# Weighted sums of two attentions with tokens on partitions, and a mask added by matmul

## The chip, the core and the metric

The kernel runs on one core of a Trainium2 chip, and the whole computation, two different network blocks one after the other, is one launch. A core has a matrix engine (TensorE: PE for the matmuls and PEld for its weight loads in the profile), a vector engine (DVE), a scalar engine (ACT), GpSimd (POOL) and a sync engine (SP) that here mostly issues DMAs. They run side by side, each through its own list of instructions in a fixed order, and wait for each other by semaphores. The metric is the device time of one execution, in microseconds (us); lower is better.

## The reference

All is in float32 with 256 tokens of width 1024. The first block (two layers of a pooling, a sparse-attention and a memory branch with mixture of experts) is touched by the change in one buffer count only. The second block has two layers; in each, a projection z = rms(x) w_in feeds three mixers whose outputs stand side by side and go through w_out, followed by a feed-forward part:

```python
# swa, 8 heads of 64 (2 heads of keys and values): window and causal by chunks of 64, with sinks
s = where(allowed, q k^T / 8, -inf);  m = max(max(s), sink);  p = exp(s - m)
ya = (p / (sum(p) + exp(sink - m))) v
# fox, 4 heads of 64: softmax attention with forget gates F
s = where(kpos <= qpos, q k^T / 8 + F_q - F_k, -inf);  yb = softmax(s) v
# mlstm, 4 heads of 64, the gated memory: by chunks in the reference
Dm = where(causal, b_t - b_s + i_s, -inf);  m_t = max(inter, max(Dm))
h = ((q k^T * exp(Dm - m_t)) v + old state) / max(|den|, exp(-m_t))
x = x + concat([ya, yb, rms(h) * gate]) @ w_out
x = x + square(relu(rms(x) @ w_ff1)) @ w_ff2
```

## The kernel before, in words

The 256 tokens are two blocks of 128, one per step of the loops over `b` (`NB` is 2). Activations have tokens on the 128 partitions; what a dense product needs is turned by PE transposes (a matmul with the identity) so that the contraction is on partitions. Dense products are done in two halves of each number: `split` makes a rounded high part `wh` and a rest `wl` of a weight (L99 and L100, or L104 and L105 with a gain), `transposed` (L174 to L177) and `split_out` (L286, L287) do the same with activations, and `mm3` multiplies high by high (L111), high weight rest by high (L112) and the rest of the activations by high (L113).

In the second block (`second_layer`, from L1228) a layer goes: the projections in pieces (`project`), the gated memory (`mlstm`, L1482 to L1545), swa (L1349 to L1386), fox (L1446 to L1479), then `w_out` with the eight blocks of input rows in the order `ks=(6, 0, 2, 4)`: the gated memory's rows first, swa's next, fox's last. With `early=True` the last parts run all of token block 0 before block 1 (`TAIL = 3`). Then the residual is added (L1270), x is turned (L174) and the feed-forward part follows. The order of the instructions on an engine is not written out: a tile scheduler orders them when the program is built, and puts dense products that are ready between the steps of the mixers.

For each token block, swa first makes the scores of all heads (L371), and one fused DVE instruction per head (L1362) adds the mask, writes the masked scores to SBUF and leaves the row's maximum. In a second loop, for each pair of heads, ACT takes the exponentials (L1380) with their sums; `over_sum` (L1388 to L1395) adds the sink's term (L1392), takes the reciprocals (L1393) and multiplies both heads' rows by them (L1395); and `weighted` (L375 to L387) turns the normalised rows with PE (L381), copies them to SBUF (L383, on ACT, or on DVE for the second pair of fox) and multiplies (L386). There a value block of 128 keys x 64 is the stationary operand and the turned probabilities stream, so that the sums come out with the head's 64 columns on partitions, two heads in one 128-partition tile: what `w_out` needs. `split_out` writes them to `yh` and `yl` (tiles named `big`). fox does the same with four heads, scores at L1460 and L1463, maxima at L1467 and exponentials at L1474. Token block 0 has 128 keys (one block of keys), token block 1 has 256 (two).

The gated memory already has its sums with tokens on partitions: transposes L1522, copy L1524, and L1529, where the turned weights are the stationary operand and the 64 value columns stream. L1533 multiplies by the reciprocal denominators, and after the norm, whose chain runs over ACT, DVE and POOL (L1198 to L1203, L1538, L1540), two transposes (L1543) turn the result back. Its exponents come from matmuls whose mask and maxima are the fused instruction at L1501, one for each head.

## Time and profile before

| | us |
|---|---|
| runs of the kernel before | 1623.46, 1632.21, 1632.83 (median 1632.21) |
| the profiled execution | 1629.87 |
| its span in the trace | 1628.1 |
| the granted clock of PE, mean over the span | 0.988 |
| second block | from about 1008 to the end |

The profile is of one execution. Its span reaches from the first instruction to the last, and 1.77 us of the execution lie around it. A row of a timeline gives a start and a length in us; successive matmuls overlap at their ends, so what a matmul costs on PE is the distance to the next start. A matmul in float32 appears as two records. "Idle before" and the name behind the arrow tell how long the engine had nothing to do and which instruction ended that.

### The profile page before, as it was taken

How to read it: one execution, taken by the hardware profiler on the slowest of the kernel's cores; microseconds unless marked ns; L12 is line 12 of the kernel's file. 1: busy time of each engine (PE TensorE's matmuls, PEld its weight loads, DVE VectorE, ACT ScalarE, POOL GpSimd, SP SyncE). 2: the span in 40 equal slices, each digit the busy share in tenths (PEclk: the TensorE clock that was granted, in tenths of full speed). 3: DMA queues.
4: the chain of work that ended last, by engine and by line, in shares of the span. 5: the costliest groups of instructions: out<-in, count | busy, mean ns of one | idle time of the engine just before them, and what ended most of it. 6: DMA issues, size and time to landing. Idle time of an engine off the chain costs nothing.

```text
span 1628.1 us, 24829 instructions
## 1 busy us (share of the span) xinstructions
PE 1584.0 (97%) x9844; PEld 1187.8 (73%) x9844; DVE 872.5 (54%) x1818; ACT 694.7 (43%) x1178; POOL 83.4 (5%) x97
## 2 busy tenths in 40 slices
PE   8999999999999999999999998999999999899998
PEld 7877998444436987999534344866988987688897
DVE  5587557411114687556512124787565568765554
ACT  5545544301003645544310012666555556655553
POOL 1000012000000000011000001130000000100000
PEclk9999999999999998999999999999999999999999
DMA  9553776899999652686899998623555554245550
GB/s 316 182 175 104 282 271 229 349 408 409 408 409 336 205 179 101 242 303 235 313 409 409 409 409 303 222 81 109 204 182 181 171 180 142 74 160 185 190 189 33
DMA packets 162560, 394.71 MB, mean 242 GB/s; under 512 B 15716, under 2 KB 21860, under 8 KB 162436
## 3 DMA queue, kind: packets, MB, share of 16 engines
q1 hardware_dynamic: 157184, 384.98, 64.8%
q0 software_dynamic: 2144, 6.91, 1.3%
q8 instruction: 78, 1.28, 0.3%
q10 hardware_dynamic: 3108, 1.16, 0.3%
q14 instruction: 46, 0.38, 0.1%
HBM read 391.97 MB, written 1.05 MB: 241 GB/s over the span
## 4 chain that ended last, share of the span: by engine, by line
PE 43%; DVE 4%; DMA 1%; ACT 1%; POOL 1%; issue 0%; SPq 0%; POOLq 0%; ACTq 0%; DVEq 0%
PE a L1016 7%; PE d L112 6%; PE d L111 6%; PE d L113 6%; PE a L111 4%; PE a L112 4%; PE a L113 4%; PE a L1037 3%; PE a L956 1%; DMA raw<-in_w_in_dram 1%; DVE wl L105 1%; PE d L1050 1%; DVE sall L1362 1%; PE a L386 1%; PE a L381 0%
## 5 line engine op out<-in xcount | busy, mean ns | idle before, releaser
L100 DVE TENSOR_TENSOR wl<-raw,wh 128x1024 fp32r<-128x1024 f32 (+1 forms) x232 | 284.0, 1226 | 220.2 <-ACT wh L99 219.6
L99 ACT CAST wh<-raw 128x1024 fp32r<-128x1024 f32 (+1 forms) x232 | 240.2, 1038 | 245.9 <-PE d L112 133.7
L111 PE MATMUL d<-big,wh 128*128 128x256 f32 (+1 forms) x976 | 277.7, 285 | 2.0 <-ACT big L176 1.1
L112 PE MATMUL d<-big,wh 128*128 128x256 f32 (+1 forms) x976 | 277.2, 284 | 1.8 <-DVE big L177 1.8
L113 PE MATMUL d<-big,wl 128*128 128x256 f32 (+1 forms) x976 | 275.7, 284 | 0.0
L105 DVE SCALAR_TENSOR_TENSOR wl<-raw,gcols,wh 128x512 fp32r<-128x512 f32 (+1 forms) x224 | 151.8, 713 | 76.4 <-ACT wh L104 76.0
L111 PEld LDWEIGHTS d<-big,wh 128*128 128x128 f32 (+1 forms) x976 | 186.1, 191 | 5.2 <-ACT big L176 1.8
L112 PEld LDWEIGHTS d<-big,wh 128*128 128x128 f32 (+1 forms) x976 | 186.1, 191 | 4.5 <-DVE big L177 2.4
L104 ACT ACTIVATE wh<-raw,gcols 128x512 fp32r<-128x512 f32 (+1 forms) x224 | 143.7, 687 | 104.6 <-PE a L113 39.1
L111 PE MATMUL d<-wh,big 128*128 128x512 f32 (+1 forms) x480 | 188.2, 393 | 0.0
L112 PE MATMUL d<-wl,big 128*128 128x512 f32 (+1 forms) x480 | 187.0, 390 | 1.1 <-DVE wl L105 0.9
L113 PE MATMUL d<-wh,big 128*128 128x512 f32 (+1 forms) x480 | 187.1, 390 | 0.2 <-DVE big L177 0.2
L113 PEld LDWEIGHTS d<-big,wl 128*128 128x128 f32 (+1 forms) x976 | 185.7, 191 | 0.4 <-issue 0.3
L1016 PE MATMUL a<-raw,xg 128*64 128x512 f32 x832 | 182.9, 592 | 0.0
L1016 PEld LDWEIGHTS a<-raw,xg 128*64 128x64 f32 x832 | 59.9, 137 | 118.1 <-issue 109.5
L1021 DVE TENSOR_TENSOR sl<-sl,a 128x512 f32<-128x512 f32 x16 | 11.0, 688 | 189.1 <-PE a L1016 172.8
L1037 PE MATMUL a<-raw,sl 128*64 128x512 f32 x480 | 107.0, 595 | 0.7 <-ACT sl L1028 0.7
L112 PEld LDWEIGHTS d<-wl,big 128*128 128x128 f32 x480 | 92.3, 192 | 18.0 <-DVE wl L105 1.5
L113 PEld LDWEIGHTS d<-wh,big 128*128 128x128 f32 x480 | 92.1, 192 | 18.2 <-issue 1.4
L111 PEld LDWEIGHTS d<-wh,big 128*128 128x128 f32 x480 | 92.2, 192 | 17.8 <-issue 2.0
L111 PE MATMUL a<-wh,s 128*128 128x512 f32 x256 | 101.3, 396 | 0.0
L112 PE MATMUL a<-wl,s 128*128 128x512 f32 x256 | 101.2, 395 | 0.0
(415 smaller groups left out, 2240.3 us busy)
## 6 DMA issues: line engine op xcount, KB each, us to landing
raw<-in_w_dram SPq DMA_DIRECT2D x328, 512.0 KB, 10.2
raw<-in_w_in_dram SPq DMA_DIRECT2D x64, 1024.0 KB, 6.3
raw<-in_w_ff_dram SPq DMA_DIRECT2D x64, 1024.0 KB, 5.4
br<-in_w_dram SPq DMA_DIRECT2D x36, 512.0 KB, 10.2
raw<-in_w_out_dram SPq DMA_DIRECT2D x16, 1024.0 KB, 5.1
raw<-in_w_br_dram SPq DMA_DIRECT2D x12, 1024.0 KB, 6.6
raw<-in_w_mem_kv_dram SPq DMA_DIRECT2D x7, 1024.0 KB, 11.6
gate<-in_w_dram SPq DMA_DIRECT2D x12, 512.0 KB, 10.2
```

The source lines that it names most:

```text
L99: nc.scalar.copy(hi, src)
L100: nc.vector.tensor_tensor(lo, src, hi, OP.subtract)
L104: nc.scalar.activation(hi[:, k], src[:, k], AF.Copy, scale=g)
L105: nc.vector.scalar_tensor_tensor(lo[:, k], src[:, k], g, hi[:, k], OP.mult, OP.subtract)
L111: mm(ps, sh, mh, start=start, stop=False)
L112: mm(ps, sh, ml, start=False, stop=False)
L113: mm(ps, sl, mh, start=False, stop=stop)
L386: nc.tensor.matmul(po[64 * e:64 * e + 64], value(e, k), pT[:, e, k], start=(k == 0), stop=(k == b))
L956: mm(ps[:, kk], part(b, k + kk), s[:, b], start=(i == 0), stop=(i == len(terms) - 1))
L1016: mm(ps[64 * a:64 * a + 64], g_[:, k, 64 * a:64 * a + 64], w[i][k // 2][:, a, k % 2], start=(k == 0), stop=(k == 7))
L1037: mm(pss[h][64 * a:64 * a + 64], hT[:, k, 64 * a:64 * a + 64], w[k][:, a, h], start=(k == 0), stop=(k == 3))
L1050: mm(acc[2 * b + h], sT[:, b * P:b * P + P], ys[h][:, i], start=False, stop=(p == 7 and i == 1))
```

## The change

In swa and fox, `weighted` gives way to `weighted_rows`: the exponentials are turned as they are, without the normalisation, and the turned rows become the stationary operand (128x128) with the 64 value columns streaming (L406 in the changed kernel), as in the gated memory. The sums of all heads then stand side by side with tokens on partitions, and `heads_out` takes the reciprocals of all the sums at once (L411), multiplies once for all heads (L413), turns the result in pieces of 128 columns (L417: four for swa, two for fox) and hands them to `split_out`. swa adds its sink terms once per token block. In the gated memory, a causal mask in bf16 is added to the diagonal 128 columns of each head's exponents by a matmul with a bf16 identity (L385, 8 per layer); one reduction per bank (L392) takes the maxima of the two heads in it; and the exponentials read the bank. The first block's tile of probabilities `p` has 3 buffers instead of 4. Some constants are also cast to bf16, among them copies that nothing reads.

```diff
-        p = self.t(pool, [P, S], F32, "p", 4)[:, :n]
+        p = self.t(pool, [P, S], F32, "p", 3)[:, :n]
...
+    def add_mask(self, sc, mask):
+
+        w = mask.shape[1]
+        for ps in sc:
+            m, n = ps.shape[1:]
+            for h in range(m):
+                self.nc.tensor.matmul(ps[:, h, n - w:], self.ident16, mask, start=False, stop=(h == m - 1))
+
+    def maxima(self, sc, N, tag):
+
+        m = sc[0].shape[1]
+        mx = self.t(N, [P, 2, m], F32, tag, 2)
+        for e in range(2):
+            self.nc.vector.tensor_reduce(mx[:, e], sc[e], AX.X, OP.max)
+        return mx
+
+    def weighted_rows(self, po, pr, b, pool, value, alt=False):
...
+        for e in range(2):
+            for k in range(b + 1):
+                nc.tensor.transpose(pt[:, e, k], pr[e][:, k * P:k * P + P], self.ident)
+        pT = self.t(pool, [P, 2, 2, P], F32, "pT", 2)[:, :, :b + 1]
+        (nc.vector.tensor_copy if alt else nc.scalar.copy)(pT, pt)
+        for e in range(2):
+            for k in range(b + 1):
+                nc.tensor.matmul(po[:, e], pT[:, e, k], value(e, k), start=(k == 0), stop=(k == b))
+
+    def heads_out(self, po, sm, heads, hi, lo, N):
+
+        nc = self.nc
+        nc.vector.reciprocal(sm, sm)
+        y = self.t(N, [P, 512], F32, "row2", 2)[:, :heads * 64]
+        nc.vector.tensor_tensor(y.rearrange("p (h d) -> p h d", d=64), po,
+                                sm[:, :, None].to_broadcast([P, heads, 64]), OP.mult)
+        ps = self.psa().rearrange("p (k c) -> p k c", k=4)
+        for k in range(heads // 2):
+            nc.tensor.transpose(ps[:, k], y[:, k * P:k * P + P], self.ident)
+        self.split_out(ps[:, 0:heads // 2], hi, lo)
...
-                self.over_sum(s[:, g], sm[:, g], sks[b][:, g])
                 v0 = 640 + 64 * (j // 2)
-                self.weighted(po[:, j], [s[:, 2 * j], s[:, 2 * j + 1]], b, N,
-                              lambda e, k: z[:, k, v0:v0 + 64])
-            self.split_out(po, yh[:, 0:4, cols], yl[:, 0:4, cols])
...
+                self.weighted_rows(po[:, 2 * j:2 * j + 2], [s[:, 2 * j], s[:, 2 * j + 1]], b, N,
+                                   lambda e, k: z[:, k, v0:v0 + 64])
+            nc.vector.tensor_tensor(sm, sm, sks[b], OP.add)
+            self.heads_out(po, sm, 8, yh[:, 0:4, cols], yl[:, 0:4, cols], N)
...
-                self.over_sum(s[:, g], sm[:, g])
-                self.weighted(po[:, j], [s[:, 2 * j], s[:, 2 * j + 1]], b, N,
-                              lambda e, k: z[:, k, 1280 + 64 * (2 * j + e):][:, :64], j == 1)
-            self.split_out(po[:, 0:2], yh[:, 4:6, cols], yl[:, 4:6, cols])
+                self.weighted_rows(po[:, 2 * j:2 * j + 2], [s[:, 2 * j], s[:, 2 * j + 1]], b, N,
+                                   lambda e, k: z[:, k, 1280 + 64 * (2 * j + e):][:, :64], j == 1)
+            self.heads_out(po, sm, 4, yh[:, 4:6, cols], yl[:, 4:6, cols], N)
...
-                                     start=True, stop=True)
+                                     start=(j == 0), stop=False)
+            self.add_mask(sc, self.causal)
+            nm = self.maxima(sc, N, "cmx")
+            nc.vector.tensor_scalar(nm, nm, 0.0, -1.0, OP.max, OP.mult)
...
-                nc.vector.tensor_tensor_reduce(s[:, h], sc[h % 2][:, h // 2], self.cz[:, S - n:], 1.0, 0.0,
-                                               OP.add, OP.max, mx[:, h:h + 1])
...
-                nc.scalar.activation(s[:, h], s[:, h], AF.Exp, bias=mx[:, h:h + 1])
+                nc.scalar.activation(s[:, h], sc[h % 2][:, h // 2], AF.Exp, bias=nm[:, h % 2, h // 2:][:, :1])
```

The change moves dense products on PE. The first place is layer 2, from the end of swa's scores into the weighted sums of its first token block. A row is the line, the operation, out<-in, the size, and a count where it repeats; `d` are the banks of dense products, `sall` the exponentials of swa. Before:

```order
L113 MATMUL d_21936<-wh_21954,big_20839 128x512
L111 MATMUL d_21936<-wh_21954,big_20838 128x512
L381 MATMUL a_21675<-ident,sall_4388_21611 128x128 x2
L112 MATMUL d_21936<-wl_21955,big_20838 128x512
L113 MATMUL d_21936<-wh_21954,big_20839 128x512
L111 MATMUL d_21937<-wh_21954,big_20838 128x512
L112 MATMUL d_21937<-wl_21955,big_20838 128x512
L386 MATMUL a_21667<-pT_21678,z_20807 64x128 x2
```

And in the changed kernel:

```order
L373 MATMUL a_21658<-akT_21496,s_4346_21377 128x256
L113 MATMUL d_21926<-wh_21930,big_20841 128x512
L111 MATMUL d_21926<-wh_21930,big_20840 128x512
L401 MATMUL a_21677<-ident,sall_4398_21617 128x128
L112 MATMUL d_21926<-wl_21931,big_20840 128x512
L113 MATMUL d_21926<-wh_21930,big_20841 128x512
L401 MATMUL a_21677<-ident,sall_4398_21617 128x128
L111 MATMUL d_21927<-wh_21930,big_20840 128x512
L112 MATMUL d_21927<-wl_21931,big_20840 128x512
L113 MATMUL d_21927<-wh_21930,big_20841 128x512
L406 MATMUL a_21673<-z_20809,pT_21680 128x64 x2
```

Between the last score and the first transposes 14 dense products stood before, of which the last two are shown; now two stand there. The other twelve stand further on.

The second place is layer 2, the end of fox's second token block (`sh` are its exponentials, `row` the product of `heads_out`, `x` the residual after `w_out`). Before:

```order
L386 MATMUL a_21873<-pT_21902,z_20807 64x128 x4
L381 MATMUL a_21913<-ident,sh_21874 128x128 x4
L112 MATMUL d_21936<-wl_22027,big_20838 128x512
L113 MATMUL d_21936<-wh_22026,big_20839 128x512
L111 MATMUL d_21936<-wh_22026,big_20838 128x512
L112 MATMUL d_21936<-wl_22027,big_20838 128x512
L113 MATMUL d_21936<-wh_22026,big_20839 128x512
L386 MATMUL a_21873<-pT_21918,z_20807 64x128 x4
L112 MATMUL d_21937<-wl_22019,big_20838 128x512
L113 MATMUL d_21937<-wh_22018,big_20839 128x512
```

And in the changed kernel:

```order
L406 MATMUL a_21865<-z_20809,pT_21891 128x64 x4
L401 MATMUL a_21899<-ident,sh_21866 128x128 x4
L406 MATMUL a_21865<-z_20809,pT_21904 128x64 x4
L417 MATMUL a_21913<-ident,row_4469_21911 128x128 x2
L174 MATMUL a_22064<-ident,x_17744 128x128 x4
L111 MATMUL d_21927<-wh_22014,big_20840 128x512
L112 MATMUL d_21927<-wl_22015,big_20840 128x512
L111 MATMUL d_21929<-wh_22018,big_20840 128x512
L113 MATMUL d_21927<-wh_22014,big_20841 128x512
```

Five dense products stood between the last transposes and their sums, and 17 behind the sums, the first five of which take no rows of fox. Now none stands between, and the 12 behind (four are shown) all take fox's rows of the second token block.

## Rows read from the trace of the kernel before

**Rows 1.** From the page: PE's line of the first part (busy us, share of the span, instructions), and the clock granted to it in 40 slices of the span, in tenths of full speed.

```profile
PE 1584.0 (97%) x9844; PEld 1187.8 (73%) x9844; DVE 872.5 (54%) x1818; ACT 694.7 (43%) x1178; POOL 83.4 (5%) x97
...
PEclk9999999999999998999999999999999999999999
```

**Rows 2.** Windows of the second block, one per row: start and end in us from the span's start, length; then busy us and instructions of PE, PEld, DVE, ACT and POOL in this order; the mean granted clock; the busy share of the DMA engines; GB/s. 1000 to 1020 is the start of the second block; 1049 to 1077 and 1349 to 1382 hold the gated memory of layers 1 and 2, 1077 to 1137 and 1382 to 1442 their two attentions.

```profile
1000.00:1020.00 20.00, 14.42 (x59) 11.07 (x56) 16.11 (x30) 12.10 (x20) 5.21 (x9) 0.83 0.51 169
1049.00:1077.00 28.00, 26.83 (x153) 21.04 (x151) 23.88 (x81) 16.70 (x36) 5.63 (x9) 1.00 0.35 118
1077.00:1137.00 60.00, 54.86 (x340) 39.89 (x341) 45.40 (x156) 39.92 (x99) 8.52 (x8) 1.00 0.26 90
1349.00:1382.00 33.00, 30.99 (x172) 23.75 (x170) 27.05 (x95) 18.92 (x41) 2.11 (x2) 1.00 0.36 127
1382.00:1442.00 60.00, 54.76 (x340) 39.42 (x341) 44.75 (x154) 39.66 (x98) 9.40 (x6) 1.00 0.27 88
```

**Rows 3.** What PE waited for from 1020 to 1136 (layer 1): PE's line and tile, the engine, line and tile waited for; us in total, how often, the longest.

```profile
PE a L381 <- DVE sall L1395: 1.9, 3, 0.9
...
PE a L1543 <- DVE chn L1540: 0.8, 1, 0.8
```

**Rows 4.** The same view from 1318 to 1442 (layer 2).

```profile
PE a L381 <- DVE sall L1395: 2.0, 3, 0.9
PE a L1543 <- DVE chn L1540: 1.4, 2, 0.9
```

**Rows 5.** Timeline of PE, layer 2, from the end of swa's scores (L371) into its weighted sums: start in us, us, engine, line, operation, out<-in, size, count, and in brackets the idle time before and what ended it. A 128x128 f32 matmul with 64 or 128 columns leaves two records.

```profile
1397.06 0.50 PE L113 MATMUL d<-wh,big 128*128 128x512 f32 x1
...
1397.63 0.39 PE L112 MATMUL d<-wl,big 128*128 128x512 f32 x1
...
1400.86 0.60 PE L381 MATMUL a<-ident,sall 128*128 128x128 f32 x2 [0.34 <-DVE sall L1395]
...
1402.38 0.44 PE L386 MATMUL a<-pT,z 128*64 128x128 f32 x4
1402.74 0.55 PE L381 MATMUL a<-ident,sall 128*128 128x128 f32 x3
...
1409.26 0.66 PE L386 MATMUL a<-pT,z 128*64 128x128 f32 x8
1409.85 0.33 PE L381 MATMUL a<-ident,sall 128*128 128x128 f32 x1
```

**Rows 6.** Timeline of PE, layer 2, the weighted sums of the gated memory's second token block (L1529) and its transposes on the way out (L1543).

```profile
1375.66 1.07 PE L1529 MATMUL a<-z,pT 128*128 128x64 f32 x8
1376.54 0.47 PE L112 MATMUL d<-wl,big 128*128 128x512 f32 x1
...
1382.03 0.44 PE L1543 MATMUL a<-ident,chn 128*128 128x128 f32 x2 [0.89 <-DVE chn L1540]
1382.30 1.04 PE L1327 MATMUL a<-ident,row 128*128 128x128 f32 x8
```

**Rows 7.** Timeline of PE, PEld and DVE, layer 2, the end of fox's second token block.

```profile
1431.48 0.42 PEld L386 LDWEIGHTS a<-pT,z 128*64 128x64 f32 x8 [0.37 <-ACT pT L383]
...
1432.07 0.66 PE L381 MATMUL a<-ident,sh 128*128 128x128 f32 x4
...
1432.48 0.48 PE L112 MATMUL d<-wl,big 128*128 128x512 f32 x1
...
1432.76 0.69 DVE L383 COPY pT<-a 128x512 f32<-128x512 f32 x1 [0.20 <-PE a L381]
...
1433.80 0.66 PE L386 MATMUL a<-pT,z 128*64 128x128 f32 x8
...
1434.39 0.19 PEld L112 LDWEIGHTS d<-wl,big 128*128 128x128 f32 x1 [0.17 <-issue]
```

**Rows 8.** Timeline of PE, PEld, DVE and ACT, layer 1, the end of the gated memory's second token block: the weight loads of L1529, the matmul after them, the product with the reciprocal denominators (L1533), and the rounding of the turned rows to their high part (L286).

```profile
1072.22 0.97 PEld L1529 LDWEIGHTS a<-z,pT 128*128 128x128 f32 x8 [0.23 <-ACT pT L1524]
...
1073.14 0.47 PE L112 MATMUL d<-wl,big 128*128 128x512 f32 x1
...
1073.37 0.42 DVE L1533 TENSOR_TENSOR chn<-a,cden 128x256 f32<-128x256 f32 x1 [0.35 <-PE a L1529]
...
1078.07 0.37 ACT L286 CAST big<-a 128x256 fp32r<-128x256 f32 x1 [1.57 <-PE a L1543]
```

**Rows 9.** The chain that ended last, in order of time, from 960 us on: start, us, engine, tile, line and count. L956 is a run of bf16 matmuls of 128x128.

```profile
963.18 2.79 PE a L956 x48
```

**Rows 10.** Groups of DVE instructions in the whole program: line, operation, out<-in, count, then busy us and mean ns of one, then idle us before them.

```profile
L1395 DVE TENSOR_SCALAR sall<-sall,asm 128x128 f32<-128x128 f32 (+1 forms) x32 | 8.9, 316 | 0.1
...
L1501 DVE CUSTOM_DVE_ANT_0 sh<-a,k 128x128 f32<-128x128 f32 (+1 forms) x16 | 4.7, 353 | 0.1
...
L1395 DVE TENSOR_SCALAR sh<-sh,bsm 128x128 f32<-128x128 f32 (+1 forms) x16 | 4.4, 317 | 0.3
...
L1200 DVE TENSOR_REDUCE arv<-junk 128x8 f32<-128x512 f32 x4 | 2.7, 681 | 0.0
```

**Rows 11.** Timeline of ACT, layer 2: the first exponential of swa.

```profile
1398.04 0.49 ACT L1380 ACTIVATE sall<-sall,amx,ary 128x128 f32<-128x128 f32 x1 [0.28 <-DVE amx L1369]
```

**Rows 12.** Timeline of ACT and PE in the first block, where an exponential (L280) and the transposes that read its tile (L381) come closest.

```profile
162.61 0.38 PE L381 MATMUL a<-ident,p 128*128 128x128 f32 x2
...
163.29 0.49 ACT L280 ACTIVATE p<-s,nb 128x256 f32<-128x256 f32 x1
```

More of the change, by code (lines that the diff above doesn't have):

```diff
@@ L333, in indexer @@
         masks = []
+        self.ident16 = self.t(M, [P, P], BF16, "id16", 1)
+        nc.scalar.copy(self.ident16, self.ident)
         cm = self.t(M, [P, S], F32, "cm", 1)
@@ L363, in indexer, with pair_scores @@
         return masks
-    def pair_scores(self, qT, cols, n, j, m, key):
+    def pair_scores(self, qT, cols, n, j, m, key, mask=None):
         sc = [self.psa()[:, 0:m * n].rearrange("p (h n) -> p h n", h=m) for _ in range(2)]
@@ L371, in pair_scores @@
                 self.nc.tensor.matmul(sc[e][:, hh], qT[r, j + hh, cols], key(j + hh, r),
-                                      start=True, stop=True)
-        return sc
+                                      start=(hh == 0 or mask is None), stop=mask is None)
+        if mask is not None:
+            self.add_mask(sc, mask)
+        return sc
+    def add_mask(self, sc, mask):
[12 more added lines that the diff above has]
+        nc = self.nc
+        pt = self.psa().rearrange("p (e k c) -> p e k c", e=2, k=2)[:, :, :b + 1]
+        for e in range(2):
[7 more added lines that the diff above has]
+    def heads_out(self, po, sm, heads, hi, lo, N):
+        nc = self.nc
+        nc.vector.reciprocal(sm, sm)
[6 more added lines that the diff above has]
+        self.split_out(ps[:, 0:heads // 2], hi, lo)
     def weighted(self, po, pr, b, pool, value, alt=False):
@@ L1161, in layer_params @@
         nc.gpsimd.tensor_scalar(fg[:, 0], fg[:, 0], 0.125, None, OP.mult)
-        sinks = self.bcast(N, I["swa_sinks_2"][l], 8, "sinks", 1, nc.scalar)
+        sinks = self.t(N, [P, 2, 8], F32, "sinks", 1)
+        nc.scalar.dma_start(sinks[:, 0], I["swa_sinks_2"][l].partition_broadcast(P))
+        nc.gpsimd.tensor_scalar(sinks[:, 1], sinks[:, 0], -1.0, None, OP.mult)
         fb = self.t(N, [P, 8], F32, "fbias", 1)
@@ L1261, in second_layer @@
             project(1024, 512)
-            self.swa(z, sw, sinks, yh, yl, N)
+            self.swa(z, sw, sinks[:, 0], yh, yl, N)
             self.fox_qk(z, fg, fx, N)
@@ L1353, in swa @@
             n = P * (b + 1)
-            mask = self.cm if b == 0 else self.swm
+            mask = self.cmf if b == 0 else self.swf
             s = self.t(N, [P, 8, n], F32, f"sall{b}", 1)
@@ L1381, in swa @@
                                          scale=rqs[b][:, h:h + 1], accum_out=sm[:, h:h + 1])
-                self.over_sum(s[:, g], sm[:, g], sks[b][:, g])
                 v0 = 640 + 64 * (j // 2)
-                self.weighted(po[:, j], [s[:, 2 * j], s[:, 2 * j + 1]], b, N,
-                              lambda e, k: z[:, k, v0:v0 + 64])
-            self.split_out(po, yh[:, 0:4, cols], yl[:, 0:4, cols])
-    def over_sum(self, s, sm, more=None):
-        nc = self.nc
-        if more is not None:
-            nc.vector.tensor_tensor(sm, sm, more, OP.add)
-        nc.vector.reciprocal(sm, sm)
-        for i in range(2):
-            nc.vector.tensor_scalar(s[:, i], s[:, i], sm[:, i:i + 1], None, OP.mult)
+                self.weighted_rows(po[:, 2 * j:2 * j + 2], [s[:, 2 * j], s[:, 2 * j + 1]], b, N,
+                                   lambda e, k: z[:, k, v0:v0 + 64])
+            nc.vector.tensor_tensor(sm, sm, sks[b], OP.add)
+            self.heads_out(po, sm, 8, yh[:, 0:4, cols], yl[:, 0:4, cols], N)
     def gate_rows(self, z, fb, ibias, N):
```

31 lines of the change are left out of this document (18 added, 13 removed).

## The prediction, made before the changed kernel ran

> **What bounds the kernel now.** The page's engine line and clock strip come first [rows 1]: PE is busy 97% of the span, at full clock nearly everywhere. The change lies in the second block, so I read its attention stretches next, two per layer [rows 2]. From 1077 to 1137, where layer 1 has its two attentions, PE is busy 54.86 of 60 us, and 54.76 of 60 in layer 2 (1382 to 1442), while DVE has 45.40 and 44.75, ACT 39.92 and 39.66. So PE sets the pace there too, and DVE, which the change relieves, is not the bound; what DVE's lateness costs stands in the waits of PE. They are small [rows 3, 4]: over both layers the weighted sums' transposes (L381) wait 1.9 + 2.0 = 3.9 us for the normalised rows of L1395, and the gated memory's last transposes (L1543) 0.8 + 1.4 = 2.2 for its rows. All that PE idles in the four stretches of [rows 2], whatever the reason, is 1.17 + 5.14 + 2.01 + 5.24 = 13.6 us. No relief of another engine can give back more, and each microsecond of new PE work has to be set against it.
>
> **The change, part by part.** Durations on PE are start to next start, since the ends overlap.
>
> *Weighted sums, form of the matmuls.* Before, a value block of 128x64 is loaded as weights and 128 columns of transposed probabilities stream through. Four such matmuls (8 records) take 1409.26 to 1409.85, 0.59 us, and two take 1402.38 to 1402.74, 0.36 [rows 5]. After, the probabilities are the weights and 64 columns stream. The gated memory does just this already: 8 records take 1375.66 to 1376.54, 0.88 us [rows 6], so 4 take some 0.44. There are 12 calls of each size (8 heads of swa and 4 of fox, two per call, in two layers; the second token block has the larger size): 12 x 0.29 + 12 x 0.08 = **+4.4 us**. Fewer columns stream, but a weight load twice as wide is what counts: the loads' busy time for 8 records goes from 0.42 us [rows 7] to 0.97 [rows 8]. The gap of 0.17 us put down to "issue" behind the old form [rows 7] is in the 0.59 already.
>
> The Trainium skill, TensorEngine Tiling (Array Packing), Performance Considerations, When to Use Tiling, speaks against this step: with 64 free columns on one side it wants those 64 as the stationary operand of a column tile, for a factor of two; by it the 12 x (0.59 + 0.36) = 11.4 us of these matmuls would double, and the step cost +11.4. The rows of both forms in this kernel decide for +4.4.
>
> *Transposes on the way out.* The sums now have tokens on partitions and are turned back: 4 transposes per token block in swa, 2 in fox. Four take 1432.07 to 1432.48, 0.41 us [rows 7], two 1382.03 to 1382.30, 0.27 [rows 6]: 4 x 0.41 + 4 x 0.27 = **+2.7 us**.
>
> *Mask of the gated memory by matmul.* 16 bf16 matmuls of 128x128. The trace of before has this form once, 48 in 2.79 us, 0.058 each [rows 9]; an f32 transpose of that size, 0.41 / 4 = 0.10, is the upper bound. That is 0.9 to 1.6, and I take **+1.2 us**, between the two since a change of type stands on either side of these matmuls. All this is PE time in a stretch that PE bounds: **+8.3 us**.
>
> *DVE.* The 48 normalisations, 8.9 + 4.4 = 13.3 us [rows 10], go. In their place come four products of 128x512, at 0.69 as the copy of that size [rows 7], and four of 128x256 at 0.42 (L1533 [rows 8]): 4.4 us. The reciprocals and sink additions, 40 on two columns, become 12 on four or eight. So DVE is busy at least 9 us less, 4.5 per layer, but DVE is not the bound: the gain is the wait that ends, L381 on L1395, **-3.9 us**. L1543 waits at the end of a chain from DVE's L1533 through ACT and POOL that the change leaves in place; a shorter queue on DVE can give back none or all of its 2.2 us, and I take half, **-1.1**.
>
> *Maxima by bank.* 16 fused add-and-maximum, 4.7 us, become 8 reductions straight from a bank of 512 or 256 elements, each at most the 0.68 of a 128x512 reduction [rows 10]: 5.4 at the most. The exponentials that follow start neither sooner nor later by more than some tenths, under dense products: nil.
>
> *New waits.* (a) Start of swa's weighted sums. Before, 14 dense matmuls stand between the last score and the first transposes, from 1397.06 on, and PE then waits 0.34 us [rows 5]. After, two dense ones are left, and the transposes need only the first exponential, which starts at 1398.04 and takes 0.49 [rows 11]. Two dense matmuls take 0.57 (1397.06 to 1397.63 at the pace of [rows 5]); 1398.53 less 1397.63 is a wait of 0.9, 0.6 more than the 0.34: **+1.2 us** in both layers. The 12 other dense products fill places further on.
> (b) End of fox, second token block. Before, five dense matmuls stand behind the transposes at 1432.07, so that the copy of the transposed probabilities (0.69 on DVE, from 1432.76) is done under them, and 17 dense ones behind the sums cover the split of the result [rows 7]. After, PE has L401, L406, L417, four transposes of x, and then 12 dense matmuls that all need fox's rows, with nothing free between. From the transposes' start to that of the sums' matmuls are 1.73 us (1432.07 to 1433.80), of them 0.41 the transposes: 1.3 open. Then the product: in the gated memory PE is through with the sums at 1073.14, the product starts at 1073.37 and takes 0.42 [rows 8]: 0.7 open. Then L286 (0.37 [rows 8]) and about as much again for L287 before the dense ones, under the four transposes of x (0.41) and the first dense ones, which need the high part alone: 0.2 open. Sum 2.2 per layer: **+4.4 us**.
> (c) fox's first token block waits in the same way, but the second block's scores lie beside it: half of the 1.3 in (b), 0.7 per layer, **+1.4 us**. The ends for (b) and (c) together are 0, if other work hides them, and 8, if both are open in full.
>
> *First block.* The tile of probabilities has 3 buffers and not 4. The nearest place: the exponential at 163.29 starts after the transposes of the tile three before, started at 162.61 and 0.38 long [rows 12]. Nil; were it bound, tenths per head. The added casts of constants fall into 1000 to 1020, where DVE is busy 16.11 of 20 us [rows 2]: nil; not covered, four of at most 0.69 [rows 7] are 2.8.
>
> **Sum**: 8.3 - 3.9 - 1.1 + 1.2 + 4.4 + 1.4 = **+10.3 us** on the profiled execution's 1629.87, which is 2.3 below the median of the three runs (1632.21): **1640 us**.
>
> **Rivals.**
> A (my forecast, chance 0.72): PE pays 8.3 for new work, gets 5 back and finds 7 of new waits; with the ends of the open terms +3 to +16, 1633 to 1646.
> B (slower, 0.13): the end of fox decides. If (b) and (c) are open in full, 8 in place of 5.8, and the clock falls there as it did in 1000 to 1020, where PE was busy 14.42 of 20 us and the granted clock averaged 0.83 [rows 2], then 0.17 x 20 = 3.4 us more are lost per layer: 10.3 + 2.2 + 6.8 = +19, 1649. For it: no free dense product is left in that place. Against: about 5 us of idle time in each 60 us left the clock at 1.00 [rows 2]. It decides above 1648.5, 18.6 over the profiled execution; without (b), (c) and the clock the sum is 4.5, so from 7 us lost per layer, where A has 2.9.
> C (faster, 0.08): DVE's lateness was behind all of PE's idle time. Then 13.6 us go, less the 8.3 of work: -5, 1625. Against it: after L1395 and L1543 half of that idle time is left, spread over waits of which the change touches few.
> D (0.04): the sums' matmuls take twice as long as before, because their weight loads, busy 2.3 times as long [rows 7, 8], are not hidden: 11.4 in place of 4.4 is +7.0 on A, 1647. The start-to-start times [rows 5, 6] speak for A. This is what the Trainium skill's rule on column tiling, cited above, comes to.
> E (the change does not do what it says, 0.03): the reductions from a bank cost more than the fused form, and the gated memory's exponentials come late, by one reduction of 0.68 in each of four token blocks, with no cover: 2.7 more than A, 1643.
>
> **Numbers.** The likeliest case gives 1640. The range takes in A, and of B and C all but their tails: 1626 to 1650. One per cent, 16 us, is about what a measurement of this kernel can tell from no change: slower means above 1648.5, faster below 1615.9. A, D, E and most of C lie within; B, with its spread, mostly above. Slower 0.12, faster 0.05, same 0.83.
>
> **What would show it.** In the changed profile the sums' matmuls should take 0.88 us for 8 records, start to start, with no "issue" gap behind; in swa the transposes should wait for DVE nowhere, and about 1 us for the first exponential; the 16 mask matmuls should take about 1 us in all; DVE should be busy some 5 us less per layer; at the end of fox PE should stand idle about 2 us. If PE idles less there than before, (b) and (c) are covered and the time comes out near 1634; if the clock in 1077 to 1137 is below 1.00, it is B.

## The result and the profile after

The changed kernel took 1643.56 us (median of 14 runs, 1636.64 to 1649.73), the kernel before 1631.87 (14 runs, 1623.18 to 1638.21): a ratio of 1.0074, 95% interval 1.0055 to 1.0092, or 9.0 to 15.0 us more. The profiled execution of the changed kernel is the one of 1636.64 us, the shortest of its 14, so its span understates the difference. One of the 12 runs of mem, an experiment below, took 4838.59 us and is in none of the ratios. From its page: the span, the engines and the clock strip, which answer to [rows 1].

```profile
span 1634.9 us, 24849 instructions
...
PE 1585.3 (97%) x9884; PEld 1191.2 (73%) x9884; DVE 864.3 (53%) x1730; ACT 697.1 (43%) x1180; POOL 86.4 (5%) x99
...
PEclk9999999999999999999999999999999999999999
```

DVE has lost 88 instructions and 8.2 us, and PE's busy time barely grew. Whole spans hide more than they show here: the two programs' first blocks are 1008.6 and 1006.6 us long at a mean granted clock of 0.98 and 0.99, and the kernel before alone varies there by 5 us (**again**, below). I therefore cut the second block at fixed instructions: from the first gate matmul (L1410 before, L1456 after) to the first feed-forward matmul, which I call the mixers, and from there to the next layer or the end, the feed-forward part. The windows of the kernel before, with the columns of [rows 2] (layer 1 mixers, feed-forward, layer 2 mixers, feed-forward):

```profile
1046.75:1135.26 88.51, 82.65 (x497) 61.85 (x497) 69.41 (x239) 55.97 (x134) 14.15 (x17) 1.00 0.31 105
1135.26:1317.65 182.39, 181.94 (x1153) 164.29 (x1154) 106.11 (x133) 92.77 (x128) 0.00 (x0) 1.00 0.52 174
1351.03:1440.89 89.86, 83.34 (x501) 61.56 (x502) 68.84 (x239) 56.84 (x135) 11.51 (x8) 1.00 0.30 100
1440.89:1628.10 187.21, 182.12 (x1152) 164.15 (x1152) 106.83 (x134) 91.43 (x126) 0.00 (x0) 1.00 0.45 152
```

And of the changed kernel:

```profile
1043.75:1139.77 96.02, 87.78 (x518) 67.14 (x517) 65.67 (x194) 57.03 (x134) 16.28 (x18) 1.00 0.29 96
1139.77:1320.03 180.26, 179.69 (x1152) 162.13 (x1153) 105.51 (x132) 92.84 (x128) 0.00 (x0) 1.00 0.54 176
1353.65:1449.78 96.13, 89.10 (x521) 67.99 (x521) 64.66 (x194) 57.21 (x135) 12.50 (x8) 1.00 0.29 93
1449.78:1634.90 185.12, 179.85 (x1152) 161.99 (x1152) 106.24 (x133) 91.46 (x126) 0.00 (x0) 1.00 0.46 154
```

The granted clock is 1.00 in all eight windows. The mixers are longer by 7.5 and 6.3 us, 13.8 in all; PE's busy time there grew by 5.1 and 5.8, its idle time by 2.4 and 0.5. DVE lost 3.7 and 4.2 us of work. And the feed-forward parts, whose instructions the change does not touch, are *shorter*, by 2.1 us each. That was not in the forecast's sum.

What PE waits for in the mixers of layer 2 (the view of [rows 4]):

```profile
PE a L417 <- DVE row L413: 1.0, 2, 0.5
PE a L401 <- ACT sall L1435: 0.9, 1, 0.9
PE a L1587 <- DVE chn L1584: 0.9, 2, 0.7
PE a L406 <- DVE ss L1246: 0.8, 1, 0.8
...
PE a L406 <- DVE pT L403: 0.5, 1, 0.5
...
PE d L111 <- ACT big L286: 0.2, 1, 0.2
```

The wait on normalised rows is gone, and the waits on the first exponential (L401), on the copy of the turned rows (the two of L406; for the longer one the profile names L1246, a short DVE instruction that ends beside the copy) and on the product (L417) are there. PE in layer 2, with the mask of the gated memory (L385), the start of swa's sums, and the first sums of 256 keys:

```profile
1369.34 0.40 PE L385 MATMUL a<-masks,ident 128*128 128x128 bf16 x4
1369.66 0.71 PE L373 MATMUL a<-s 64*128 64x256 f32 x3
...
1401.25 0.33 PE L401 MATMUL a<-ident,sall 128*128 128x128 f32 x1 [0.88 <-ACT sall L1435]
...
1402.69 0.59 PE L406 MATMUL a<-z,pT 128*128 128x64 f32 x4
1403.12 0.39 PE L401 MATMUL a<-ident,sall 128*128 128x128 f32 x2
...
1410.64 1.03 PE L406 MATMUL a<-z,pT 128*128 128x64 f32 x8
1411.51 0.72 PE L401 MATMUL a<-ident,sall 128*128 128x128 f32 x5
```

Eight records of L406 take 0.87 us and four 0.43, against 0.59 and 0.36 [rows 5]; a mask matmul takes 0.32 / 4 = 0.08. Where two groups stand together, 16 records, it is 1.02 us before and 1.80 after:

```profile
1105.65 1.09 PE L386 MATMUL a<-pT,z 128*64 128x128 f32 x16
1106.67 0.55 PE L1444 MATMUL a<-ident,row 128*128 128x128 f32 x3
```

```profile
1412.85 2.00 PE L406 MATMUL a<-z,pT 128*128 128x64 f32 x16
1414.65 0.48 PE L113 MATMUL d<-wh,big 128*128 128x512 f32 x1
```

So eight more records cost 0.43 us in the old form and 0.93 in the new one: inside a group the new form costs twice as much, and in a whole group of eight 1.5 times. Beyond its eight records a group of the old form takes 0.16 us (0.59 less 0.43), one of the new form nothing (0.87 for 0.93). The end of fox in layer 2, PE, DVE and ACT, which answers to [rows 7]:

```profile
1440.97 0.61 PE L401 MATMUL a<-ident,sh 128*128 128x128 f32 x4
1441.61 0.69 DVE L403 COPY pT<-a 128x512 f32<-128x512 f32 x1 [0.98 <-PE a L401]
...
1442.36 1.10 PE L406 MATMUL a<-z,pT 128*128 128x64 f32 x8 [0.78 <-DVE ss L1246]
...
1443.50 0.42 DVE L413 TENSOR_TENSOR row<-a,bsm 128x256 f32<-128x256 f32 x1 [0.94 <-PE a L406]
1443.98 0.44 PE L417 MATMUL a<-ident,row 128*128 128x128 f32 x2 [0.52 <-DVE row L413]
1444.26 0.60 PE L174 MATMUL a<-ident,x 128*128 128x128 f32 x4
1444.46 0.37 ACT L286 CAST big<-a 128x256 fp32r<-128x256 f32 x1 [2.64 <-PE a L417]
...
1444.88 0.50 PE L111 MATMUL d<-wh,big 128*128 128x512 f32 x1
```

PE has nothing between L401 and L406 and between L406 and L417, as the order said; the listed idle times are 0.78 and 0.52.

### The profile page after: what moved, and what is told of

Read it like the earlier page. It is cut to its first block, busy times and chain, and to the rows that moved or that the text cites. A ratio compares the mean times of both kernels' runs of the same rounds, so it can differ in the third digit from the quotient of the medians.

```text
span 1634.9 us, 24849 instructions
## 1 busy us (share of the span) xinstructions
PE 1585.3 (97%) x9884; PEld 1191.2 (73%) x9884; DVE 864.3 (53%) x1730; ACT 697.1 (43%) x1180; POOL 86.4 (5%) x99
## 4 chain that ended last, share of the span: by engine, by line
PE 45%; DVE 3%; ACT 1%; POOL 1%; DMA 1%; issue 0%; SPq 0%; ACTq 0%; POOLq 0%; DVEq 0%
PE a L1061 7%; PE d L113 6%; PE d L111 6%; PE d L112 6%; PE a L113 4%; PE a L112 4%; PE a L111 4%; PE a L1082 3%; PE a L1001 1%; PE a L406 1%; PE d L1095 1%; DVE wl L105 1%; DMA raw<-in_w_in_dram 1%; PE a L401 0%; POOL ary L1259 0%
## 5 line engine op out<-in xcount | busy, mean ns | idle before, releaser
L112 PEld LDWEIGHTS d<-big,wh 128*128 128x128 f32 (+1 forms) x976 | 184.2, 189 | 4.7 <-DVE big L177 2.6
L111 PEld LDWEIGHTS d<-big,wh 128*128 128x128 f32 (+1 forms) x976 | 184.0, 189 | 4.5 <-issue 1.3
L113 PE MATMUL d<-wh,big 128*128 128x512 f32 (+1 forms) x480 | 185.4, 388 | 0.2 <-DVE big L177 0.2
L112 PEld LDWEIGHTS d<-wl,big 128*128 128x128 f32 x480 | 91.4, 191 | 17.6 <-issue 1.2
```

The lines of the kernel that those rows point to most:

```text
L111: mm(ps, sh, mh, start=start, stop=False)
L112: mm(ps, sh, ml, start=False, stop=False)
L113: mm(ps, sl, mh, start=False, stop=stop)
```

## The experiments

The lengths in us of the mixers (layers 1, 2) and the feed-forward parts (1, 2), read as above, for every kernel of this study. Each row is one profiled execution:

| kernel | mixers | feed-forward |
|---|---|---|
| before | 88.5, 89.9 | 182.4, 187.2 |
| changed | 96.0, 96.1 | 180.3, 185.1 |
| again | 88.6, 89.9 | 182.4, 187.1 |
| mem | 91.8, 89.8 | 180.2, 184.9 |
| rows | 95.8, 97.2 | 180.3, 184.9 |
| swarows | 92.8, 94.6 | 179.9, 184.6 |
| nonorm | 86.6, 88.5 | 182.5, 187.5 |
| normback | 95.5, 97.1 | 180.1, 184.9 |
| d406 | 100.2, 100.3 | 180.3, 184.8 |
| noturn | 92.8, 92.8 | 179.9, 184.8 |
| shift | 88.6, 91.4 | 180.0, 184.5 |
| align | 88.6, 91.3 | 180.7, 185.4 |
| place | 88.5, 89.9 | 182.1, 186.8 |
| place2 | 88.7, 90.0 | 178.5, 183.3 |

Six of these mixers did not run at full clock throughout. In mem (layer 1), rows (both layers), normback, shift and align (layer 2 each) the granted clock lay at the lower of its two levels, 1.2 in place of 2.4 GHz, for 3.4 us. Two of these stretches, of shift and of rows, in the columns of [rows 2]:

```profile
1405.32:1408.73 3.41, 3.41 (x16) 2.24 (x16) 3.03 (x13) 2.69 (x6) 0.00 (x0) 0.50 0.00 0
1448.25:1451.66 3.41, 2.89 (x12) 2.41 (x12) 1.32 (x3) 0.96 (x2) 0.00 (x0) 0.50 0.02 5
```

What it cost can be read where the order of PE's instructions is the same at full clock. shift (the kernel before with an unused buffer), layer 2, and then the kernel before:

```profile
1404.80 0.63 PE L381 MATMUL a<-ident,sall 128*128 128x128 f32 x4 [0.94 <-DVE sall L1396]
...
1405.64 0.63 PE L112 MATMUL d<-wl,big 128*128 128x512 f32 x1
1406.07 0.63 PE L113 MATMUL d<-wh,big 128*128 128x512 f32 x1
...
1409.24 0.48 PE L112 MATMUL d<-wl,big 128*128 128x512 f32 x1
```

```profile
1407.76 0.63 PE L381 MATMUL a<-ident,sall 128*128 128x128 f32 x4 [0.94 <-DVE sall L1395]
...
1408.47 0.40 PE L112 MATMUL d<-wl,big 128*128 128x512 f32 x1
1408.70 0.40 PE L113 MATMUL d<-wh,big 128*128 128x512 f32 x1
...
1410.70 0.48 PE L112 MATMUL d<-wl,big 128*128 128x512 f32 x1
```

The dense product takes 0.43 us in place of 0.23, and the whole stretch 4.44 in place of 2.94: 1.5 us. Up to there the two programs run within 0.1 us of each other, and behind it the distance stays. Read in the same way, against a program or a layer with the same order at full clock, the fall cost 1.5 us in mem, 1.4 and 1.0 in rows, 1.4 in normback and 1.3 in align. The wait of 0.94 us in front of it stands in the kernel before too, where the clock stayed at 1.00; so I take these 1.0 to 1.5 us off below, where the edits are compared. Why the clock fell there and not elsewhere, and whether it would again in a second execution of these programs, is open.

**again**, the kernel before without an edit.

> The kernel before, unchanged, profiled once more, to see how far two executions of one program differ stage by stage. The stretch from the gate matmuls (L1410) to the first feed-forward matmul was 88.5 us in layer 1 and 89.9 in layer 2 of the first trace (96.0 and 96.1 in the changed kernel's). If that length is a property of the program, it comes out within 0.5 us again. The feed-forward part, the same in both programs, was 182.4 and 187.2 us before and 180.3 and 185.1 after: if that is a matter of the execution and not of the change, it will be found to vary here too by about 1%.

The mixers came out within 0.1 us and the feed-forward parts within 0.2, while the first block took 1013.8 us in place of 1008.6. So at full clock the stage lengths of the second block belong to the program, and what the feed-forward parts lose is no matter of the execution.

**mem** and **rows**, the two halves of the change (mem: `over_sum` and `weighted` put back into swa and fox; rows: the fused mask and maxima put back into the gated memory).

> The gated memory's part of the change alone (mask by matmul, maxima by bank, the bf16 casts, three buffers for the first block's probabilities); swa and fox as before. Theory A (PE's work decides, and this part adds only 16 small matmuls): 0 to +1 us per layer in the stretch from the gate matmuls to the first feed-forward matmul, +0 to +2 us in all, ratio 1.000 to 1.002. Rival E (the reductions come late and hold up the exponentials): +1.5 us or more per layer, ratio 1.002 or more.

> The weighted sums of swa and fox with tokens on partitions, divided once; the gated memory as before. Theory A: nearly the whole of the slowdown, +6 us per layer in the stretch from the gate matmuls to the first feed-forward matmul, ratio 1.006 to 1.008. Rival E: less than half of it, ratio below 1.004.

mem: 1630.58 against 1630.75 us, ratio 0.9995 (0.9976 to 1.0014). rows: 1642.39, ratio 1.0068 (1.0048 to 1.0088), mixers +7.3 in both layers, of which the clock has 1.4 and 1.0: +5.9 and +6.3, theory A's +6. The weighted sums are the slowdown; the gated memory's part has none that can be measured in the whole time. Its mixers are 3.3 us longer in layer 1 and unchanged in layer 2, and the feed-forward parts are 2.2 and 2.4 shorter. Of the 3.3, 1.0 is a longer wait for swa's normed keys (2.1 us on L1397 in layer 1 of both mem and the changed kernel, 1.1 before) and 1.5 the clock; the remaining 0.8 was not traced further.

**swarows**, the kernel of rows with `over_sum` and `weighted` put back into fox as well.

> Weighted sums with tokens on partitions in swa alone; fox and the gated memory as before. The stretch from the gate matmuls to the first feed-forward matmul was 88.5 and 89.9 us before, 95.8 and 97.2 with both attentions changed (the run of the rows part). Theory A, by its terms per layer: form of the matmuls +1.5, transposes +0.8, wait for the first exponential +0.6, waits on normalised rows -1.9: swa +1 to +2.5, and the rest (some 5 us per layer) is fox with its uncovered end. Rival W (each new group of small matmuls costs where it breaks a run of dense ones, wherever it stands): shares as the calls, 8 of 12, so swa +4.5 or more per layer.

+4.3 and +4.7, at full clock: swa has about three quarters of the 5.9 and 6.3, a little more than its share of the calls (8 of 12). Theory A's +1 to +2.5 for swa fell. One term that failed can be seen: the waits on L1395 (3.9 us in both layers, all of them swa's) are gone, yet PE's listed idle time in the mixers is 14.4 us where the kernel before has 12.1. In their place PE waits for the first exponential (0.9 per layer) and, further on, for copies, for the rounding of the turned rows and for the residual. Rival W's reason (a cost at each break in a run of dense products) was not tested by itself; the dense products, 405 in number as before, take 1.3 us more from start to next start.

**nonorm** and **normback** take the division away from the kernel before, and put it back into the changed one:

```diff
 nonorm (before)
-                self.over_sum(s[:, g], sm[:, g], sks[b][:, g])
...
-                self.over_sum(s[:, g], sm[:, g])
...
 normback (changed)
+                self.over_sum(s[:, 2 * j:2 * j + 2], sm[:, 2 * j:2 * j + 2], sks[b][:, 2 * j:2 * j + 2])
...
+                self.over_sum(s[:, g], sm[:, g])
...
-        nc.vector.tensor_tensor(y.rearrange("p (h d) -> p h d", d=64), po,
-                                sm[:, :, None].to_broadcast([P, heads, 64]), OP.mult)
+        nc.vector.tensor_copy(y.rearrange("p (h d) -> p h d", d=64), po)
```

> The kernel before without the sums' reciprocals and the multiplication of the rows (L1392 to L1395): it leaves out the division in swa and fox, so the sums are not normalised. No matmul is added or removed. It is the ceiling of what a lighter DVE can give. Theory A: only the waits of the transposes on L1395 end, -1.9 us per layer, or less as the exponentials are the next to be waited for (-1 to -2 per layer, ratio 0.998 to 0.999). Rival C (DVE's lateness is behind most of PE's idle time): -4 us or more per layer, ratio 0.995 or less.

> The changed kernel with the rows normalised before the sums as they were (the additions of the sinks, the reciprocals and the 48 multiplications back on DVE), and a plain copy in place of the product with the reciprocals. PE's instructions are those of the changed kernel. Theory A: the waits on normalised rows come back, +1 to +2 us per layer in the stretch from the gate matmuls to the first feed-forward matmul. Rival (with PE as the bound the lighter DVE was worth nothing): within 0.3 us per layer.

nonorm: 0.9968 (0.9944 to 0.9991), mixers -1.9 and -1.4. That is all that a lighter DVE gives when nothing else is changed: the waits on L1395 go and one of 0.9 us on the first exponential remains. normback: -0.5 and +0.9 against the changed kernel; in layer 2 the clock cost 1.4, so -0.5 in both. Putting the division back lengthens nothing, against theory A's +1 to +2. What PE waits for there, layer 2:

```profile
PE a L415 <- DVE row L412: 1.8, 3, 0.8
PE a L406 <- DVE pT L403: 0.8, 1, 0.8
PE a L406 <- ACT pT L403: 0.7, 1, 0.7
PE a L401 <- DVE sall L1448: 0.7, 1, 0.7
```

The wait on normalised rows (L1448) is back with 0.7 us only, where the changed kernel waits 0.9 for the first exponential. Both versions have the way behind the transposes, copy and product; that this way decides is argued from the waits and not tested by itself. (A variant's instructions are ordered anew when it is built, so these are not the same order with one wait more.)

**d406**, each group of L406 twice, and **noturn**, which leaves out the transposes L417:

```diff
 d406
+        for _ in range(2):
             for e in range(2):
...
 noturn
-        for k in range(heads // 2):
-            nc.tensor.transpose(ps[:, k], y[:, k * P:k * P + P], self.ident)
-        self.split_out(ps[:, 0:heads // 2], hi, lo)
+        self.split_out(y.rearrange("p (k c) -> p k c", c=P), hi, lo)
```

> The changed kernel with each group of the sums' matmuls (L406) issued twice, the second over the first. Their price by the rows of before, 0.88 and 0.44 us for 8 and 4 records, 6 calls of each per layer: +7.9 us per layer in the stretch from the gate matmuls to the first feed-forward matmul, less what now covers a wait (up to 1 us). If their wide weight loads were hidden behind other work the price would be that of the old form or less, +5.7 us per layer.

> The changed kernel without the transposes on the way out (L417): the product with the reciprocals is written to the high and low tiles as it lies, unturned, so w_out multiplies the wrong layout. It leaves out the turning of the results of swa and fox. Theory A: the transposes (1.4 us of PE per layer) and the wait of PE for the product at the end of fox and in its first block (1.0 us) go: -2 to -2.5 us per layer in the stretch from the gate matmuls to the first feed-forward matmul. If PE's gaps absorb the transposes, as they absorbed nearly half of the doubled sums: -1 us.

In d406, 48 records run from 1110.30 to 1115.57, 0.11 each, the same price as in the changed kernel:

```profile
1110.30 5.47 PE L407 MATMUL a<-z,pT 128*128 128x64 f32 x48
1115.57 0.47 PE L112 MATMUL d<-wl,big 128*128 128x512 f32 x1
```

The sums' matmuls take 15.9 us of PE in layer 1 in place of 8.3, +7.6, yet the mixers grow by 4.2 in either layer, less than either case expected. Of the rest, 1.5 us is listed idle time of PE that is gone (6.3 and 5.0 us listed, for 7.8 and 6.5); the remainder is spread over other matmuls, whose order is another. noturn gives back 3.3 us per layer, more than the 2.0 to 2.5 expected for the transposes (1.5) and their wait (1.0). So a microsecond put in or taken out on PE, its wait included, was worth between 0.55 and 1.3 us of length here: PE sets the pace, but not to the microsecond. How much of L406's price is weight load and how much streaming was not separated.

**The feed-forward parts.** All programs with the change's constants have them short. Their matmuls run closer together. PE, layer 2, 35 matmuls of the up-projection before, and 36 after the change:

```profile
1445.78 0.28 PE L112 MATMUL d<-big,wh 128*128 128x256 f32 x1
...
1449.98 0.28 PE L111 MATMUL d<-big,wh 128*128 128x256 f32 x1
```

```profile
1451.78 0.28 PE L111 MATMUL d<-big,wh 128*128 128x256 f32 x1
...
1456.02 0.28 PE L111 MATMUL d<-big,wh 128*128 128x256 f32 x1
```

4.20 / 35 = 0.120 and 4.24 / 36 = 0.118 us. The new bf16 masks and identity and the wider tile of sinks add 1312 bytes per partition ahead of `z` and the `big` tiles. **shift** adds just these, unused:

```diff
         k2 = self.C2.tile([P, 896], F32, name="k2")
+        self.C2.tile([P, 328], F32, name="spare")
```

> The kernel before with a tile of 1312 bytes per partition that nothing reads or writes, among the second block's constants. It moves the buffers behind it (the big tiles, z, the weights' partners) to the addresses they have in the changed kernel, and does nothing else; no instruction differs. Three programs with the change's buffers (both parts, memory part, rows part) had feed-forward parts of 180.2 and 185 us, three without them 182.4 and 187.2. Theory P (the place of the big tiles in SBUF: their start is 0 modulo 64 bytes where it was 32): feed-forward shorter by 2.1 us per layer, its 256-column matmuls at 117 ns in place of 120, and the dense products between the mixers' steps at 233.5 ns in place of 228 (+1 us per layer in the stretch from the gate matmuls to the first feed-forward matmul): -2 to -3 us in all, ratio 0.998 to 0.999. Rival (some instruction of the change does it): nothing moves, ratio 1.000.

The feed-forward parts came as theory P said, -2.4 and -2.7, ratio 0.9978 (0.9959 to 0.9997). The mixers are +0.1 and +1.6, and the 1.6 is the clock's 1.5 and 0.1: theory P's +1 us per layer for the slower pace of their dense products did not come. The gain belongs to the place of the buffers and not to any instruction. **align** and **place** tried which property of the place it is, with unused tiles of 32 and 96 bytes at five places:

> The kernel before with tiles of 32 bytes that nothing uses at five places (in front of the residual, of the expert part, of the second block's constants, around its big tiles and before its weights), so that the operands of the dense products start at 0 modulo 64 bytes in both blocks; the other operands stay where they are. No instruction differs. Theory P as for the run with one tile, in both blocks: some 1900 256-column matmuls of the first block and 1536 of the second at 117 ns in place of 120, -10 us; the 512-column ones, whose streamed operand moves too, unknown: between -5 ns and +5 ns each for some 2200, -11 to +11 us. If both operands at 0 are good for these too: -10 us or more, ratio 0.994 or less. If the 512-column matmuls lose as they did between the mixers' steps: about -5 us.

> The kernel before with unused tiles of 32 and 96 bytes at the five places of the run with 64-byte starts, so that all operands of the dense products start at 0 modulo 128 bytes. No instruction differs. So far: streamed operands of 256 columns at 0 modulo 128 ran at 117 ns, at 32, 64 and 96 at 120. Theory Q (the start of the streamed operand modulo 128 decides): 117 ns in the first block too, and the 256-column matmuls give -5.5 us there and -4.3 in the feed-forward parts, ratio 0.994 or less unless the 512-column ones lose 5 ns each (+5 us). Rival (the distance between the two operands decides, which is 0 modulo 128 here as it was in the slow cases): 120 ns everywhere, ratio 1.000.

align: 0.9972 (0.9957 to 0.9987), but with the 256-column matmuls at 120 ns: theory P's reason (a start at 0 modulo 64) fell, and the gain came from the 512-column ones of the feed-forward parts. place: 1.0013 (0.9993 to 1.0033); theory Q fell as well, the rival held. What is left is the distance between the two operands of a matmul. The mean time between starts in runs of dense matmuls (from the fifth of a run on; by which runs are counted, a mean moves by up to 1 ns), against the start of the stationary operand less that of the streamed one, modulo 512 bytes, as each program was laid out:

| distance | 256 columns | 512 columns |
|---|---|---|
| 0 | 120.0 (before, first block), 120.0 (place) | 228.5 (before, first block), 228.3 (place, mixers) |
| 256 | 119.9 (before, feed-forward) | 228.1 (before, mixers) |
| 128 | 119.7 (align) | 232.5 (place, feed-forward) |
| -128 | | 232.7 (align, mixers) |
| -32 | 117.0 (changed), 116.7 (shift) | |
| 32, 64 | | 233.5, 233.3 (changed: mixers, feed-forward) |
| 288 | | 233.2 (before, feed-forward) |
| -64 | | 228.9 (align, feed-forward) |

The start of one operand alone does not decide. In the first block the streamed operand starts at 64 modulo 512 in align and in place2 (below), and the stationary one at 32 in the kernel before and in place2; the 256-column matmuls take 120 ns in align and before, and 117 in place2.

**place2** sets the best of these, -32 for 256 columns in both blocks and -64 for the feed-forward's 512, in the kernel before:

```diff
+        self.t(self.RB, [P, 8], F32, "padb", 1)
...
+        self.t(self.wp, [P, 120], F32, "padw", 1)
...
+        self.t(self.M, [P, 8], F32, "padm", 1)
...
+            self.t(E, [P, 8], F32, "pad", 1)
...
             z = self.t(N, [P, NB, 2572], F32, "z", 1)
+            self.t(N, [P, 72], F32, "pad", 1)
             hT = self.transposed([x[:, b] for b in range(NB)], N)
+            self.t(N, [P, 96], F32, "pad2", 1)
```

> The kernel before with unused tiles that set the distance between the two operands of the dense products (start of the stationary less start of the streamed one, modulo 512 bytes) to the values that ran fastest so far. 256-column matmuls: -32 in both blocks (117 ns in the run with one spare tile; 120 at 0 and at 128). 512-column ones of the feed-forward parts: -64 (228.9 ns in the run with 64-byte starts; 232.5 to 233.3 at other distances). The price: the 512-column ones of the first block and of the second block's projections and w_out come to +32 (233 ns in place of 228). No instruction differs. Theory D (the distance decides, in both blocks): some 1900 matmuls of the first block -3 ns and 576 +5 ns, feed-forward 1536 at -3 and 768 at -4.4, mixers +1.9 us as in the run with one spare tile: -5.7 + 2.9 - 4.6 - 3.4 + 1.9 = -9 us, ratio 0.993 to 0.996. Rival (other buffers that moved along made the difference): first block unchanged at 120 ns, -3 us or less in all, ratio 0.998 or more.

1625.26 against 1631.27 us, ratio 0.9955 (0.9935 to 0.9976): faster than the kernel before, and so than the changed one, without an instruction changed. The paces came as theory D gave them: 117.0 and 116.7 ns for 256 columns in the two blocks, 228.9 for the feed-forward's 512, and 233 to 234 for those at +32. The feed-forward parts are 3.9 us shorter each; the mixers are 0.2 and 0.1 longer, where theory D had 1.9 in all, so the slower pace of their dense products costs them next to nothing in this order. Its up-projection, layer 2, 35 matmuls in 4.08 us, 0.117 each:

```profile
1448.83 0.28 PE L112 MATMUL d<-big,wh 128*128 128x256 f32 x1
...
1452.91 0.28 PE L114 MATMUL d<-big,wl 128*128 128x256 f32 x1
```

## Why the prediction was right, and where it was not

The total was right: +10.3 us forecast, +11.7 between the medians, and "same", within 1%, as the likeliest. That it came so close is in part luck: the mixers grew by 13.8 us, 3.5 more than forecast, and the feed-forward parts, which the sum did not have, gave back 4.2. The mixers by kinds, both layers, from start to next start less listed idle time (each gap above 0.15 us), against the terms:

| term | forecast | measured |
|---|---|---|
| form of the sums' matmuls | +4.4 | +5.5 (16.6 for 11.2) |
| transposes on the way out | +2.7 | +3.0 |
| mask matmuls | +1.2 | +1.3 |
| PE's idle time (all waits, old and new) | +2.0 | +2.2 (14.3 for 12.1) |
| dense matmuls, 405 in number | 0 | +2.3 |
| other small matmuls | 0 | -0.5 |
| feed-forward parts | 0 | -4.2 |

The measured terms add up to +9.6. The rest of the 11.7 was not traced; the interval, 9.0 to 15.0, holds both. No run has the first block's three buffers by themselves, so that the term put at nothing for them stays open.

- *PE sets the pace, the new work on it costs.* Right in direction and nearly in size. Its largest term was a little too small: 16.6 us of L406 for 15.8 forecast, 11.2 of L386 for 11.4. The doubling that rival D stood for did not come: 16.6 is 1.5 times 11.2. So the Trainium skill, TensorEngine Tiling (Array Packing), Performance Considerations, When to Use Tiling, is right here about the direction (64 as the stationary side of a column tile is the cheaper form); its factor of two shows inside a group (0.93 us for 0.43) but not for the sums as a whole, whose groups are short.
- *The wait that ends is the gain, -3.9.* This step failed. The waits on L1395 did end, and in the kernel before their removal is worth 3.3 us (nonorm). But in swarows PE's idle time rose without them (14.4 us for 12.1), and in the changed kernel putting the division back made the mixers no longer (normback, -0.5 in both layers). That rows which are ready earlier only wait further on, for the copy, the matmul and the product in line behind the transposes, is the likely reason; the lists of waits fit it, and no run tests it alone. The 1.1 us expected back on the gated memory's last transposes did not come: they wait 2.2 us as before (1.3 + 0.9), with 3.7 and 4.2 us less work on DVE for the 4.5 forecast.
- *New waits.* (a) 0.9 us on the first exponential in both layers, as read. The sum took the 0.34 us of the first transposes off twice, in the 3.9 and again in "0.6 more"; with +1.8 in place of +1.2 it would have been +10.9. (b) 0.78 + 0.52 = 1.3 us listed at the end of fox per layer for 2.2; by the prediction's own measure, start to start less the transposes, it is 1.0 + 0.7 + 0.2 = 1.9. (c) 0.5 + 0.5 for 0.7. A layer-1 wait for swa's keys, 1.0 us longer, was not foreseen.
- *Where it falls.* The working gave swa little and fox's end most. Measured at full clock, swa alone adds 4.3 and 4.7 us (swarows) of the 5.9 and 6.3 of both attentions (rows).
- *Buffers cost nothing by where they lie.* Costing the added constants at nothing was wrong: the shift by 1312 bytes sped up the feed-forward parts by 4.2 us. It also slowed the mixers' dense matmuls in unbroken runs from 228 to 233 ns, but in shift and place2 that lengthened the mixers by 0.2 us a layer at the most. Without it the changed kernel would have been some 4 us slower still, an estimate from the feed-forward parts; what the slower pace costs in its own order was not tried.
- *The rivals.* B: no clock fell in the changed kernel's profiled execution (1.00 in both mixers). In that of rows it fell in both layers, once at fox's end, as B had it, but cost 1.4 and 1.0 us and not 3.4. C: the ceiling, nonorm, is 3.3 us, not 13.6. E: mem's ratio is 0.9995; the eight reductions take 2.6 + 1.5 = 4.1 us for the fused 4.7.

## What to carry to other kernels

Relieving an engine that is not the bound gave less here than the waits on it showed (3.3 of 3.9 us), and nothing once more steps stood in line behind; price that chain, and look whether anything is left to run under its end. Compare two programs stage by stage, between instructions that both have, and look at stages that the change should not touch: there the second effect shows. Look at the granted clock of each stage first: a fall of 3.4 us was worth as much as some of the effects looked for. A change that adds or resizes a buffer moves all buffers behind it, so time it against the old kernel with a dummy of that size.

## What the runs showed of the hardware

Matmuls in unbroken runs depend on where their operands lie to each other in SBUF: 117 or 120 ns for 256 columns, 228 to 229 or 232 to 234 for 512, at full granted clock, with nearly the same pace (within 1 ns) wherever the same distance occurred in these programs. The rule behind the distances is open: only those in the table were tried, the distance modulo 512 was read off after the fact in all runs but place2, and a cause (banks, the weight loads, other engines' writes) was not tested.

In the attentions the granted clock fell to its lower level in some profiled executions and not in others with the same order of instructions on PE (shift and align against the kernel before, place and place2): 3.4 us at 0.50 cost 1.0 to 1.5 us, in six of the 28 mixers read here.

Weighted sums of 128 keys with 64 value columns: eight more records in a group cost 0.43 us with the values as the stationary operand (128x64, 128 columns streaming) and 0.93 with the probabilities (128x128, 64 columns streaming); whole groups of eight cost 0.59 and 0.87.
